# A two-layer hybrid block on one core: the RWKV scan's inverses laid out head outermost, its u through two PSUM banks, and the first modulation in parts of 768 and 512 tokens without GpSimd

## The chip, the cores and the metric

The kernel runs on one core of a Trainium2 chip. The metric is the device time of one execution in microseconds; three executions of the kernel before took 3964.69, 3973.21 and 3976.9 us (median 3973.21). In what follows, PE is TensorE (PEld its weight loads), DVE is VectorE, ACT is ScalarE, POOL is GpSimd, and SP is SyncE, which issues most of the transfers.

## The reference, cut to what matters

Two layers of a diffusion transformer work on 256 context and 1024 latent tokens of width 1024. Layer 0 mixes the tokens with an mLSTM and with RWKV-7, layer 1 with HGRN-2 and latent attention. Only the entry of layer 0 and the RWKV-7 recurrence are touched here:

```
hj = concat([modulate(rmsnorm(xc, g), shc_a, scc_a),      # 256 context tokens
             modulate(rmsnorm(x, g),  sh_a,  sc_a)])      # 1024 latent tokens
modulate(h, shift, scale) = h * (1 + scale) + shift       # per feature
feat = hj @ w_in                                          # 3984 columns
# RWKV-7, both directions, 8 heads of 64:
sa = S @ a_t
S  = S * w_t + sa b_t^T + v_t k_t^T
y_t = S @ r_t
```

The kernel computes the recurrence in chunks of 64 tokens. Within a chunk the values `sa` of all tokens depend on each other through a triangular system; its inverse, one 64x64 matrix for each head, chunk and direction, is prepared ahead of the scan.

## The kernel before, in words

The program is one long list of instructions written through a tile framework. The framework gives every tile a buffer of its pool's tag (so many buffers for each tag), orders the instructions of each engine by a priority, which follows the order in the source, and by a simulation of when each is ready, and puts semaphores between engines. The engines then work through their lists strictly in order. Two accesses to one PSUM bank by different engines are put one behind the other, even if they touch different partitions. `weave` interleaves generators: it takes one segment of each in turn, and a segment ends at a `yield`.

*The entry (lines 606 to 640).* `scaled` loads the tokens in batches of 2, 4 and 4 tiles of 128, scales each token by its norm (line 317), and transposes it on PE (line 619) into `xT`, features on partitions, tokens along the row. For each batch there are eight PSUM evictions, one for each block `k` of 128 features, all on DVE (lines 621 and 623). Beside it `ada` computes the shift and the scale of each feature (`modT`, `AT`, lines 257 and 271). The tokens are then modulated in two halves of 640. For each of the eight blocks `k` of a half: the context tokens are modulated on DVE (line 635), the latent ones on ACT (line 637); DVE rounds the result to the high part `hh` (line 639); GpSimd, or DVE where `k % 3 == 2`, subtracts it to give the low part `hl` (line 640). Every product with weights is then made of three matmuls, `hh*wh`, `hh*wl` and `hl*wh` (lines 286 to 288).

*Weights.* `prefetch` takes the next 128 columns of the input weights: a load on SP into the tile `raw` (line 280, one buffer), the high part `wh` on ACT (line 281), and the low part `wl`, here on DVE (line 282); the split tiles have two buffers. Both first prefetches stand between the two halves of the tokens. `weights` hands out what is ready and prefetches more.

*The first features.* The features 12, 13, 14, 4, 0 and 8 come first, for the first 640 tokens. Each takes two PSUM tiles (tag "ps", four buffers): tokens 0 to 256, and tokens 256 to 642 (`PART`, with two neighbours for a mean over tokens). Only then come tokens from 639 on.

*The scan (lines 983 to 1141).* Two generators, `scan(1)` and `scan(0)`, one for each direction, are woven with the remaining modulation matmuls (line 245). PSUM has tags `ch` (three buffers), `am` (three), `ps` (one) and `mo` (one). In each of ten steps `load` fetches one tile of 128 tokens (two chunks): among others the inverses `XB` (line 1017), whose two heads of a pair lie on the partitions 0 to 63 and 64 to 127, each in its own 64 of 128 columns, with zeros beside them. For each chunk: `pr` (lines 1086 and 1087) and its copy `rs` on DVE (1089); `pu`, the inverses times `rs`, eight matmuls in the source, for four pairs of heads and two heads of a pair (line 1094); the copy of `pu` into `uv`, the partitions 0 to 63 on DVE (1096) and 64 to 127 on ACT (1097); the new state `pz` (1105 and 1106) with its sum, decay and copies (1108 to 1117); the output `py` (1125 and 1127). `pr`, `pu`, `pz` and `py` all use the tag `ch`. Between them stand parts of the preparation of the next step's matrices, `products` (1034 to 1044) and `turn` (1052 to 1056, whose three copies into `KB` are on ACT). When a tile has got both directions, `finish` normalizes it (1151 to 1165).

The lines of the change:

Of the kernel before, what the change touches and what calls it, by code (L numbers as in the profile page):

```python
# [10 lines left out]
F32 = mybir.dt.float32  # L11
F32R = mybir.dt.float32r
AF = mybir.ActivationFunctionType
ALU = mybir.AluOpType
# [3 lines left out]
P = 128  # L18
# [5 lines left out]
T = NCTX + NLAT  # L24
# [131 lines left out]
def _body(tc, nc, I, out, dbg, stop, es):  # L156
    V, S, G, TE, SY = nc.vector, nc.scalar, nc.gpsimd, nc.tensor, nc.sync
# [3 lines left out]
    def nm(p):  # L161
        _n[0] += 1
        return f"{p}_{_n[0]}"
# [11 lines left out]
    def ps(w=512, tag="ps"):  # L175
        pool, bufs = banks[tag]
        t = pool.tile([P, 512], F32, tag=tag, name=nm("ps"), bufs=bufs)
        return t if w == 512 else t[:, :w]
# [4 lines left out]
    def dram(shape, name):  # L183
        return tc.dram_tile(list(shape), F32, name=name)
# [369 lines left out]
    xcd = dram([2, P, 20, 4, 64], "xcd")  # L554
# [11 lines left out]
    with ExitStack() as ph:  # L566
        lay = ExitStack()
        hp = ph.enter_context(tc.tile_pool(name="hp", bufs=1, reuse_waits="tile"))
        hh = hp.tile([P, KD, T], F32R, name="hh")
        hl = hp.tile([P, KD, T], F32R, name="hl")  # L570
# [20 lines left out]
        def prefetch():  # L591
            c0 = feats.pop(0)
            ready.append(wsplit(I["ev_w"][:, c0:c0 + P].rearrange("(k p) c -> p k c", p=P), [P, KD, P], pool=wp, bufs=2, rbufs=1, leng=V))
# [7 lines left out]
        with tc.tile_pool(name="np", bufs=2, side="right", reuse_waits="tile") as npool:  # L601
            xT = npool.tile([P, KD, T], F32, name="xT", bufs=1)

            def scaled():

                for src, i0, n, t0 in ((I["xc"], 0, 2, 0), (I["x"], 0, 4, 256), (I["x"], 4, 4, 768)):
                    xs = []
                    for i in range(n):
                        xt = npool.tile([P, D], F32, tag="xt", name=nm("xt"), bufs=4)
                        SY.dma_start(xt, src[(i0 + i) * P:(i0 + i + 1) * P, :])  # L610
                        xs.append(xt)
                    yield
                    for i, xt in enumerate(xs):
                        norm_scale(npool, xt, xt, xT[:, :, t0 + i * P:t0 + (i + 1) * P])
                    yield
                    for k in range(KD):
                        pt = ps()
                        for i, xt in enumerate(xs):
                            TE.transpose(pt[:, i * P:(i + 1) * P], xt[:, k * P:(k + 1) * P], ident)
                        if k % 2:  # L620
                            V.tensor_copy(xT[:, k, t0:t0 + n * P], pt[:, :n * P])
                        else:
                            V.tensor_copy(xT[:, k, t0:t0 + n * P], pt[:, :n * P])
                        if k % 2:
                            yield
            weave(scaled(), ada(0, npool, [0], 4))
            for t0, t1 in ((0, T // 2), (T // 2, T)):
                if t0:
                    prefetch()
                    prefetch()  # L630
                for k in range(KD):
                    for c0, c1, v in ((t0, max(t0, NCTX), 1), (max(t0, NCTX), t1, 0)):
                        m, b, f = AT[:, 0, 0, k, v:v + 1], modT[:, 0, k, v:v + 1], xT[:, k, c0:c1]
                        if v and c1 > c0:
                            V.tensor_scalar(f, f, m, b, op0=ALU.mult, op1=ALU.add)
                        elif c1 > c0:
                            S.activation(f, f, AF.Identity, bias=b, scale=m)
                    f = xT[:, k, t0:t1]
                    V.tensor_copy(hh[:, k, t0:t1], f)  # L639
                    (V if k % 3 == 2 else G).tensor_tensor(hl[:, k, t0:t1], f, hh[:, k, t0:t1], op=ALU.subtract)  # L640
        H = T // 2

        PART = (((0, 256, 0, 0, 256, 1, 1), (256, 386, 256, 0, 384, 1, 0)), ((639, 322, 0, 1, 320, 0, 0), (958, 322, 320, 2, 320, 0, 1)))
# [340 lines left out]
    with ExitStack() as ph:  # L984
        sb = ph.enter_context(ExitStack())
        sb.enter_context(psum(ch=3, am=3, ps=1, mo=1))
        rp = scans.enter_context(tc.tile_pool(name="rp", bufs=1, side="right", reuse_waits="tile"))
# [3 lines left out]
        yfd = dram([NT, P, 4, P], "yfd")  # L991
        hfd = dram([NT, P, 512], "hfd")

        XB = [[rp.tile([P, 2, 4, P], F32, name=f"XB{d}{i}") for i in range(2)] for d in range(2)]
        ZB = [[rp.tile([P, 4, P], F32, name=f"ZB{d}{i}") for i in range(2)] for d in range(2)]
        for t_ in XB[0] + XB[1] + ZB[0] + ZB[1]:
            G.memset(t_, 0.0)
# [3 lines left out]
        def scan(d):  # L1001
            bst4 = strict.unsqueeze(1).to_broadcast((P, 4, 64))

            def load(step):
                c = ORD[d][step]
                xb = XB[d][step % 2]
                CM = rp.tile([P, 4, 3, P], F32, tag="CM", name=nm("CM"), bufs=4)
                BK = rp.tile([P, 4, 2, 2, 64], F32, tag="BK", name=nm("BK"), bufs=3)
                ZV = rp.tile([P, 2, 2, 4, 64], F32, tag="ZV", name=nm("ZV"), bufs=4)
                SY.dma_start(CM[0:64, :, 0:2, :], ard[d][c, 0:64])  # L1010
                SY.dma_start(CM[64:128, :, 1:3, :], ard[d][c, 64:128])
                SY.dma_start(BK, bkd[d][c])
                for e in range(2):
                    q = slice(64 * e, 64 * e + 64)
                    SY.dma_start(ZV[64 - 64 * e:128 - 64 * e, :, e].rearrange("p c f v -> p c (f v)"),
                                 vtd[d][c * P:(c + 1) * P, e].rearrange("(c t) f v -> t c (f v)", c=2))
                    SY.dma_start(xb[q, :, :, 64 * e:64 * e + 64].rearrange("p c f t -> p (c f) t"),
                                 xcd[d, q, 2 * c:2 * c + 2].rearrange("p c f t -> p (c f) t"))
                return dict(c=c, xb=xb, CM=CM, BK=BK, ZV=ZV)

            def amat(o):
# [49 lines left out]
            for step in range(NT):  # L1071
# [4 lines left out]
                c, xb, CM, ZV, AM, KB = (cur[k] for k in ("c", "xb", "CM", "ZV", "AM", "KB"))  # L1076
                first = step < ORD[1 - d].index(c) or (step == ORD[1 - d].index(c) and d == 0)
                yt = rp.tile([P, 4, P], F32, tag=f"yt{d}", name=nm("yt"), bufs=2)
                for cc in range(2):
                    tk = slice(64 * cc, 64 * cc + 64)  # L1080
                    last = step == NT - 1 and cc == 1
                    uv, zb = ZV[:, cc], ZB[d][zi % 2]
# [5 lines left out]
                    rs = rp.tile([P, 4, 64], F32, tag="rs", name=nm("rs"), bufs=2)  # L1088
                    V.tensor_copy(rs, pr.rearrange("p (f v) -> p f v", f=4))
                    yield  # L1090
                    pu = ps(256, tag="ch")
                    for f in range(4):
                        for e in (0, 64):
                            TE.matmul(pu[e:e + 64, f * 64:f * 64 + 64], xb[:, cc, f, e:e + 64], rs[:, f, :], start=True, stop=True)
                    puv = pu.rearrange("p (f v) -> p f v", f=4)
                    V.tensor_copy(uv[0:64, 0], puv[0:64])
                    S.copy(uv[64:128, 1], puv[64:128])
                    if parts:
                        parts.pop(0)()
                    yield  # L1100
                    if not last:
# [5 lines left out]
                        t1 = rp.tile([P, 4, 64], F32, tag="t1", name=nm("t1"), bufs=2)  # L1107
# [77 lines left out]
        def gates_ml():  # L1185
# [90 lines left out]
            yield  # L1276

        weave((gates_ml(), 1, 0), (scan(1), 1, 0), (scan(0), 1, 0), (mods, 0.6, 0))
        scans.close()
        sb.close()  # L1280
# [167 lines left out]
    with both as ph:  # L1448
# [5 lines left out]
        for f in (4, 5, 6, 7, 8, 9, 10, 11, 0, 1, 2, 3):  # L1454
# [7 lines left out]
            for r in runs[1:] if f < 4 else runs:  # L1462
                pt = held.pop(1) if f == F0 and r in runs[:2] else od_run(w, *r)
                next(mods, None)
                t0, n = r[:2]
# [8 lines left out]
            else:  # L1474
                d = f // 4 - 1
# [544 lines left out]
```

## Time and profile before

| what | value |
|---|---|
| median of three executions | 3973.21 us (3964.69 to 3976.9) |
| the profiled execution | 3966.18 us, span 3964.4 us |
| PE busy | 3620.1 us, 91% |
| DVE, ACT, POOL busy | 57%, 35%, 38% |
| mean granted clock of PE | 0.956 |
| 0 to 90 us: loading, scaling and modulating the first tokens | PE full only from about 89 us |
| 768 to 1082 us: the scan | PE busy 261.88 of 314 us |

The page of the profile has the busy time of each engine, the span in 40 slices with the busy share of each in tenths, and the costliest groups of instructions by line. A view of stretches gives the busy time of each engine in each stretch of time, the granted clock and the share of time the transfers were busy. A row of a group has the line, the engine, the operation, out and in, the shapes, the count, the busy time and the mean of one in ns, and the idle time of the engine ahead of it with what ended it. A row of waits reads: who waited for whom, us in total, times, longest. A row of the timeline starts with the start and the length in us. The view of one line gives the shortest, the median and the longest of its instructions in ns. Times count from the start of the span.

### The profile page before, as it was taken

Reading aid. Unit: us, or ns where it says so; the run is one execution under the profiler, and the core shown is the slowest. Engines: PE = TensorE matmul, PEld = TensorE weight load, DVE = VectorE, ACT = ScalarE, POOL = GpSimd, SP = SyncE. Lnnn points to the kernel's source line nnn. Section 1 sums busy time; section 2 is a strip of 40 time slices with the busy share of each in tenths; the row PEclk is TensorE's granted clock in tenths of the full one; section 3 lists DMA queues with packets and bytes.
Section 4 is the critical chain, followed back from the end, with each engine's and each line's share of the span. In section 5 each row is a group of like instructions: output and inputs, shape, how many; then the busy total and the mean of one; then the engine's idle time right before and its main releaser. Section 6 shows DMA issues by size and latency. Waiting matters only on the chain.

```text
span 3964.4 us, 66839 instructions
## 1 busy us (share of the span) xinstructions
PE 3620.1 (91%) x26934; PEld 3104.0 (78%) x26934; DVE 2266.7 (57%) x3627; ACT 1368.7 (35%) x2641; POOL 1506.0 (38%) x1532
## 2 busy tenths in 40 slices
PE   5999989888778799999999989989888979999998
PEld 3888879766667598998999878986666758888887
DVE  6564653355566656556655542227777466666655
ACT  3444342355533432123312142224444444223221
POOL 3044646433343443233323231234455544333332
PEclk7999999899889899999999999999999989999999
DMA  4555646779587633223222266322122364334332
GB/s 169 125 136 127 158 124 160 186 196 247 165 288 238 213 91 96 75 80 117 76 74 80 70 205 203 114 94 89 61 81 84 101 206 123 101 96 139 95 101 75
DMA packets 534911, 521.32 MB, mean 132 GB/s; under 512 B 128297, under 2 KB 443625, under 8 KB 534601
## 3 DMA queue, kind: packets, MB, share of 16 engines
q1 hardware_dynamic: 438904, 441.03, 38.1%
q10 hardware_dynamic: 82080, 35.17, 3.1%
q0 software_dynamic: 13616, 40.84, 2.9%
q8 instruction: 212, 3.47, 0.4%
q14 instruction: 99, 0.80, 0.1%
HBM read 395.79 MB, written 121.16 MB: 130 GB/s over the span
## 4 chain that ended last, share of the span: by engine, by line
PE 51%; DVE 6%; POOL 4%; DMA 3%; issue 2%; ACT 2%; POOLq 0%; SPq 0%; DVEq 0%; ACTq 0%
PE ps L286 16%; PE ps L287 16%; PE ps L288 16%; POOL tb L1685 1%; DMA raw<-in_mlp_w 1%; DVE KQ L1690 1%; DVE el L1883 1%; POOL wl L282 1%; POOL acc L1885 0%; PE ps L245 0%; DVE acc L504 0%; ACT wh L281 0%; DMA y<-yd 0%; POOL mh L338 0%; PE ps L1848 0%
## 5 line engine op out<-in xcount | busy, mean ns | idle before, releaser
L281 ACT CAST wh<-raw 128x1024 fp32r<-128x1024 f32 x330 | 340.9, 1049 | 1002.0 <-PE ps L288 497.4
L286 PE MATMUL ps<-mh,wh 128*128 128x384 f32 (+2 forms) x1888 | 631.2, 334 | 4.7 <-ACT mh L337 3.0
L288 PE MATMUL ps<-mh,wl 128*128 128x256 f32 (+2 forms) x1888 | 627.6, 332 | 3.3 <-POOL wl L282 3.3
L287 PE MATMUL ps<-mh,wh 128*128 128x256 f32 (+2 forms) x1888 | 627.6, 332 | 0.0
L471 DVE TENSOR_TENSOR relu<-relu 128x384 f32<-128x384 f32 (+1 forms) x192 | 332.9, 1734 | 398.8 <-ACT relu L470 398.7
L282 POOL TENSOR_TENSOR wl<-raw,wh 128x1024 fp32r<-128x1024 f32 x145 | 350.9, 2421 | 534.7 <-ACT wh L281 533.2
L286 PE MATMUL ps<-wh,h1h 128*128 128x512 f32 x1152 | 451.1, 392 | 5.4 <-ACT acc L502 2.7
L288 PE MATMUL ps<-wh,h1l 128*128 128x512 f32 x1152 | 449.9, 391 | 0.0
L287 PE MATMUL ps<-wl,h1h 128*128 128x512 f32 x1152 | 449.6, 390 | 0.0
L504 DVE TENSOR_TENSOR acc<-ps,acc 128x512 f32<-128x512 f32 x540 | 359.4, 685 | 153.8 <-PE ps L288 151.0
L473 POOL TENSOR_TENSOR h1l<-relu,h1h 128x384 fp32r<-128x384 f32 (+1 forms) x192 | 202.8, 1056 | 531.1 <-DVE h1h L472 527.4
L286 PEld LDWEIGHTS ps<-mh,wh 128*128 128x128 f32 x1888 | 358.2, 190 | 39.0 <-issue 11.1
L288 PEld LDWEIGHTS ps<-mh,wl 128*128 128x128 f32 x1888 | 358.0, 190 | 23.7 <-POOL wl L282 3.8
L287 PEld LDWEIGHTS ps<-mh,wh 128*128 128x128 f32 x1888 | 358.0, 190 | 21.6 <-POOL mh L338 0.3
L282 DVE TENSOR_TENSOR wl<-raw,wh 128x1024 fp32r<-128x1024 f32 x185 | 235.9, 1299 | 210.3 <-ACT wh L281 190.1
L288 PE MATMUL ps<-hh,wl 128*128 128x256 f32 (+2 forms) x992 | 315.8, 318 | 14.6 <-DVE wl L282 14.6
L286 PE MATMUL ps<-hh,wh 128*128 128x256 f32 (+2 forms) x992 | 324.4, 327 | 3.6 <-DVE hh L639 3.6
L287 PE MATMUL ps<-hl,wh 128*128 128x256 f32 (+2 forms) x992 | 317.7, 320 | 5.4 <-POOL hl L640 5.0
L286 PEld LDWEIGHTS ps<-wh,h1h 128*128 128x128 f32 x1152 | 216.8, 188 | 50.8 <-DVE acc L504 3.7
L288 PEld LDWEIGHTS ps<-wh,h1l 128*128 128x128 f32 x1152 | 216.8, 188 | 45.3
L287 PEld LDWEIGHTS ps<-wl,h1h 128*128 128x128 f32 x1152 | 216.9, 188 | 43.5 <-DVE wl L282 0.2
L288 PEld LDWEIGHTS ps<-hh,wl 128*128 128x128 f32 x992 | 192.9, 194 | 15.9 <-DVE wl L282 15.4
(533 smaller groups left out, 7288.9 us busy)
## 6 DMA issues: line engine op xcount, KB each, us to landing
raw<-in_mlp_w SPq DMA_DIRECT2D x256, 512.0 KB, 4.0
adaw<-in_ada_w SPq DMA_DIRECT2D x96, 512.0 KB, 4.5
raw<-in_ev_w SPq DMA_DIRECT2D x46, 512.0 KB, 4.0
bkd<-BK SPq DMA_DIRECT2D x16, 640.0 KB
CM<-ard SPq DMA_DIRECT2D x40, 256.0 KB, 9.1
BK<-bkd SPq DMA_DIRECT2D x20, 512.0 KB, 8.6
qk<-qkd SPq DMA_DIRECT2D x20, 512.0 KB, 7.9
fk<-fkd SPq DMA_DIRECT2D x20, 512.0 KB, 4.3
```

The source lines that it names most:

```text
L281: S.copy(h, raw)
L282: (leng or G).tensor_tensor(l, raw, h, op=ALU.subtract)
L286: TE.matmul(o, lh, rh, start=first, stop=False)
L287: TE.matmul(o, lh, rl, start=False, stop=False)
L288: TE.matmul(o, ll, rh, start=False, stop=last)
L471: V.tensor_tensor(r_, r_, r_, op=ALU.mult)
L473: G.tensor_tensor(l_[:, t0:t1], r_, a[:, t0:t1], op=ALU.subtract)
L504: V.tensor_tensor(acc[i][:, cs_], pt, acc[i][:, cs_], op=ALU.add)
L1685: G.tensor_tensor(nx, cb[:, :, 0], cb[:, :, 1], op=ALU.mult)
L1690: V.tensor_tensor(o, o, w, op=ALU.mult)
L1883: (V, V, V, G)[k % 4].tensor_tensor(el, e, eh, op=ALU.subtract)
```

## The change

It has three edits. (1) In the entry, the evictions of odd blocks move from DVE to ACT; the tokens are modulated in parts of 768 and 512 instead of 640 and 640; one prefetch stands ahead of the first part and one ahead of the second; the high parts are rounded on ACT except where `k % 4 == 3`, which stay on DVE; all the subtractions are on DVE. (2) The tile `XB` has the head outermost, so that what one partition loads for one head is one piece of 2 KB, where it was eight of 256 bytes. The zeros beside it stay zero. (3) The products of the two heads of a pair go to two PSUM tiles, one of tag `ch` and one of tag `ps`; DVE reads one, ACT the other.

```diff
                         if k % 2:
-                            V.tensor_copy(xT[:, k, t0:t0 + n * P], pt[:, :n * P])
+                            S.copy(xT[:, k, t0:t0 + n * P], pt[:, :n * P])
                         else:
                             V.tensor_copy(xT[:, k, t0:t0 + n * P], pt[:, :n * P])
...
-            for t0, t1 in ((0, T // 2), (T // 2, T)):
+
+            prefetch()
+            for t0, t1 in ((0, 768), (768, T)):
                 if t0:
-                    prefetch()
                     prefetch()
                 for k in range(KD):
...
                     f = xT[:, k, t0:t1]
-                    V.tensor_copy(hh[:, k, t0:t1], f)
-                    (V if k % 3 == 2 else G).tensor_tensor(hl[:, k, t0:t1], f, hh[:, k, t0:t1], op=ALU.subtract)
+                    if k % 4 == 3:
+                        V.tensor_copy(hh[:, k, t0:t1], f)
+                    else:
+                        S.copy(hh[:, k, t0:t1], f)
+                    V.tensor_tensor(hl[:, k, t0:t1], f, hh[:, k, t0:t1], op=ALU.subtract)
...
-        XB = [[rp.tile([P, 2, 4, P], F32, name=f"XB{d}{i}") for i in range(2)] for d in range(2)]
+        XB = [[rp.tile([P, 2, 2, 4, 64], F32, name=f"XB{d}{i}") for i in range(2)] for d in range(2)]
...
-                    SY.dma_start(xb[q, :, :, 64 * e:64 * e + 64].rearrange("p c f t -> p (c f) t"),
-                                 xcd[d, q, 2 * c:2 * c + 2].rearrange("p c f t -> p (c f) t"))
+                    SY.dma_start(xb[q, e].rearrange("p c f t -> p (c f t)"), xcd[d, q, 2 * c:2 * c + 2].rearrange("p c f t -> p (c f t)"))
...
-                    pu = ps(256, tag="ch")
+
+                    pus = [ps(256, tag=t_).rearrange("p (f v) -> p f v", f=4) for t_ in ("ch", "ps")]
                     for f in range(4):
-                        for e in (0, 64):
-                            TE.matmul(pu[e:e + 64, f * 64:f * 64 + 64], xb[:, cc, f, e:e + 64], rs[:, f, :], start=True, stop=True)
-                    puv = pu.rearrange("p (f v) -> p f v", f=4)
-                    V.tensor_copy(uv[0:64, 0], puv[0:64])
-                    S.copy(uv[64:128, 1], puv[64:128])
+                        for e, pu in enumerate(pus):
+                            TE.matmul(pu[64 * e:64 * e + 64, f], xb[:, e, cc, f, :], rs[:, f, :], start=True, stop=True)
+                    V.tensor_copy(uv[0:64, 0], pus[0][0:64])
+                    S.copy(uv[64:128, 1], pus[1][64:128])
```

## The prediction

> **What bounds the kernel now.** I read the page first, then the prologue and the scan in stretches of time, their waits and their groups of instructions. TensorE (PE) carries the kernel, so an edit is worth what it takes from PE's idle time in its own stage.
>
> ```profile
> PE 3620.1 (91%) x26934; PEld 3104.0 (78%) x26934; DVE 2266.7 (57%) x3627; ACT 1368.7 (35%) x2641; POOL 1506.0 (38%) x1532
> PE   5999989888778799999999989989888979999998
> ```
>
> The slices (99 us each) dip at the start, where the first tokens are modulated, and in slices 8 to 13, of which 8 to 11 hold the scan. The diff touches just these two places. First the prologue; columns are busy time of PE, PEld, DVE, ACT, POOL, then granted clock and DMA share:
>
> ```profile
> 56.50:69.50 13.00, 1.14 (x2) 0.58 (x2) 13.00 (x21) 11.39 (x16) 7.29 (x5) 0.55 0.01 1
> 69.50:72.00 2.50, 0.00 (x0) 0.00 (x0) 2.50 (x2) 0.00 (x0) 1.39 (x1) 0.50 0.00 0
> 72.00:76.20 4.20, 4.18 (x24) 4.18 (x25) 4.20 (x4) 0.24 (x1) 3.75 (x3) 0.65 0.46 125
> 76.20:89.10 12.90, 8.22 (x26) 5.27 (x26) 12.86 (x19) 1.29 (x2) 8.90 (x5) 0.72 0.15 41
> 89.10:97.50 8.40, 8.40 (x50) 8.40 (x50) 3.86 (x7) 2.94 (x5) 0.00 (x0) 0.83 0.29 79
> 97.50:104.60 7.10, 7.10 (x51) 7.10 (x50) 3.34 (x5) 2.01 (x4) 0.00 (x0) 1.00 0.30 76
> ...
> PE ps L288 <- DVE wl L282: 10.8, 1, 10.8
> ...
> PE ps L287 <- POOL hl L640: 5.0, 5, 1.3
> ...
> PE ps L286 <- DVE hh L639: 3.6, 2, 3.1
> ```
>
> VectorE (DVE) is busy without a break from 56.5 to 89.1 while PE mostly waits. The first feature needs 24 matmuls over 256 columns and 24 over 386 (tokens 256 to 642). The former run from 72.0 to 76.2, since the first weights' low part (L282) comes behind the whole first half of tokens. The latter need tokens past 640, so they crawl to 89.1 behind the second half. From 89.1 PE is full, and a feature takes 7.1 us at full clock. Why DVE is so slow:
>
> ```profile
> L639 DVE CAST hh<-xT x16: 479/482/1857, 58.3 to 85.9; 128x640 fp32r<-128x640 f32 x16
> ...
> L635 DVE TENSOR_SCALAR xT<-xT,AT,modT x8: 400/1016/1634, 57.7 to 69.1; 128x256 f32<-128x256 f32 x8
> ...
> L639 DVE CAST hh<-xT 128x640 fp32r<-128x640 f32 x16 | 13.8, 905 | 0.0
> L635 DVE TENSOR_SCALAR xT<-xT,AT,modT 128x256 f32<-128x256 f32 x8 | 7.9, 1016 | 0.0
> L282 DVE TENSOR_TENSOR wl<-raw,wh 128x1024 fp32r<-128x1024 f32 x2 | 5.1, 2558 | 0.0
> L640 DVE TENSOR_TENSOR hl<-xT,hh 128x640 fp32r<-128x640 f32 x4 | 3.2, 812 | 0.0
> ...
> L640 POOL TENSOR_TENSOR hl<-xT,hh 128x640 fp32r<-128x640 f32 x12 | 21.3, 1786 | 16.1 <-DVE hh L639 16.1
> ...
> L282 DVE TENSOR_TENSOR wl<-raw,wh 128x1024 fp32r<-128x1024 f32 x185 | 235.9, 1299 | 210.3 <-ACT wh L281 190.1
> ```
>
> The same cast takes 0.48 or 1.86 us, the same scaling 0.40 or 1.63, and L282 2.56 here against 1.30 over the run. The long ones are those beside GpSimd's twelve subtractions. Against minima and means that is (0.905-0.48)x16 + (1.016-0.40)x8 + (2.558-1.299)x2 = 14 us of DVE time in this stretch.
>
> **The prologue after the change.** ScalarE (ACT) has these rows to price its new work; L1054 is a PSUM copy of the scan, taken as the nearest row for an eviction:
>
> ```profile
> 50.87 1.05 ACT L281 CAST wh<-raw 128x1024 fp32r<-128x1024 f32 x1 [1.30 <-DMA raw<-in_ev_w]
> 56.50 11.39 ACT L637 ACTIVATE xT<-xT,modT,AT 128x384 f32<-128x384 f32 x16 [4.38 <-DVE AT L271]
> ...
> L637 ACT ACTIVATE xT<-xT,modT,AT 128x640 f32<-128x640 f32 x8 | 6.6, 906 | 0.0
> L637 ACT ACTIVATE xT<-xT,modT,AT 128x384 f32<-128x384 f32 x8 | 4.9, 694 | 4.4 <-DVE AT L271 4.4
> ...
> L1054 ACT COPY KB<-ps 128x512 f32<-128x512 f32 x20 | 11.7, 586 | 1.6 <-PE ps L1052 1.0
> ...
> L621 DVE COPY xT<-ps 128x512 f32<-128x512 f32 x8 | 5.5, 685 | 1.1 <-PE ps L619 1.1
> ```
>
> Evictions: 12 of 24 go from DVE to ACT. In the last batch of tokens that is 4x0.59 = 2.4 us of ACT, in the 4.38 us that it idles before L637, and 4x0.685 = 2.7 us off DVE, where the scales (L271) stand behind most of the copies. I take 1 us of that as gain (bounds 0 and 2.7: the transposes may set the pace). The first 8 lie beside loads; nothing taken.
>
> First part, 768 tokens, on DVE: one L282 1.3, eight scalings 8x0.40 = 3.2, two casts of 768 2x0.48x768/640 = 1.2, eight subtractions 8x0.812x768/640 = 7.8: 13.5 us. On ACT: two L637 rows give 0.83 ns a column, so eight of 512 cost 8x0.80 = 6.4, and six casts of 768 (1.05 less 256 columns) 6x0.84 = 5.0: 11.4 us. DVE sets the pace. It began at 56.5 and now begins at 55.5, plus 1 us until the first cast from ACT arrives: the part is ready at 70, where it was ready before with 640 tokens. No GpSimd runs, so the short durations hold.
>
> PE takes the 256-column matmuls with DVE, token block by token block, instead of behind it; the last pair ends at 70.5. The 386-column ones then have all their tokens: 386/642 of 7.1 = 4.3 us at full clock, 8.5 at half. PE will have been busy some 30% of the time before (4.2 us of matmuls in 13.5), and a dense start got 0.65 over its first 4.2 us (72.0 to 76.2), which leaves 4.3-2.7 = 1.6 us for after: 5.8 us, end 76.3. The second feature follows at full clock until 83.4, against 97.5 before. Gain **14 us**. Bounds: 0, if DVE and ACT wait for each other at each block (below); 19, if the overlap of consecutive DVE instructions and the evictions each give 2 us more and the clock is full.
>
> The Trainium skill, page "TensorE: Matmul & The Clock Gate", section "What's actually happening", says that half rate is the idle state and that one busy window of about 3.4 us brings full rate; the 0.65 above agrees. Should the paced stretch count as busy there, the 386-column matmuls would run at full rate at once and the gain were 15.5.
>
> The later part, 512 tokens, is 8x0.65 + 2x0.39 = 6 us of DVE and 8x0.80 + 6x0.63 = 10.2 us of ACT. It is hidden under six features at tokens below 642, 6x7.1 = 43 us of PE; without that cover it would cost its 10 us. On ACT and DVE the features' own evictions queue behind it, but four PSUM buffers hold two features. Weights: of the two loads issued between the parts one now stands ahead of the first; its DMA and cast ran ahead already (50.87), so only its L282 moves, past the whole first part. The raw tile has one buffer, so the second load waits on SP for that L282, now some 15 us earlier; nothing is moved past POOL's queue. After the prologue PE is the bound (7.10 of 7.10), so I carry the gain to the end.
>
> **The scan after the change.**
>
> ```profile
> 768.00:1082.00 314.00, 261.88 (x4484) 205.68 (x4484) 166.31 (x364) 166.28 (x353) 111.41 (x111) 0.91 0.80 208
> ...
> ACT ZV L1097 <- DVE ZV L1096: 44.0, 22, 8.1
> ...
> PE ps L1105 <- DVE ZV L1096: 10.1, 3, 3.9
> ...
> PE ps L1094 <- ACT ZV L1097: 3.1, 3, 1.0
> PE ps L1105 <- ACT ZV L1097: 3.1, 3, 1.0
> ...
> L1096 DVE COPY ZV<-ps 64x256 f32<-64x256 f32 x40 | 16.5, 414 | 21.6 <-PE ps L1094 18.2 <-ACT KB L1056 2.3 <-ACT ZV L1097 0.3
> ...
> 904.27 1.15 PE L1094 MATMUL ps<-rs,XB 128*64 128x64 f32 x32
> 905.07 0.88 DVE L1096 COPY ZV<-ps 64x256 f32<-64x256 f32 x2 [0.82 <-PE ps L1094]
> ...
> 905.58 0.83 ACT L1097 COPY ZV<-ps 64x256 f32<-64x256 f32 x2 [4.78 <-DVE ZV L1096]
> ```
>
> Both copies of u read one bank, and ACT's waits for DVE's. Two banks let it start 0.414 + 0.1 (905.58 less the first copy's end) = 0.5 us earlier. But ACT's 44 us of waiting are not PE's: PE waits six times for L1097, and the three long waits for L1096 stay. Six times 0.5 is 3 us; 44.0 us of ACT counted 22 times at 0.5 bounds it at 11.
>
> The change adds a wait. The second bank is the tag "ps", one buffer, and both directions use it. The second direction's matmuls into it wait until the first's L1097 has read it: u of both was one run of 32 matmuls in 1.15 us, and now a gap of about 0.1+0.37+0.1 = 0.57 stands in its middle (0.83 for two of ACT's copies is 0.37 each with 0.1 between). Behind it in PE's queue are the state's products (L1105) and the modulation matmuls. Where the rounds' u's are back to back, that costs 0.1 to 0.6; in others the second one is later anyway. I take 8 of 20 rounds at 0.3 = 2 us. Bounds: 0 and 24 (below). Net gain 1 us.
>
> The XB load has 256-byte pieces and 128 KB, and becomes 2 KB pieces:
>
> ```profile
> ZV<-vtd SPq DMA_DIRECT2D x35, 128.0 KB, 7.7
> ...
> XB<-xcd SPq DMA_DIRECT2D x36, 128.0 KB, 7.7
> ```
>
> ZV of the same size with 1 KB pieces lands as late, so I take 0. The Trainium skill, "DMA: Bandwidth & Descriptors", section "Specifications", puts line rate at 512 bytes and more; these two rows show no such difference in landing.
>
> **Sum.** The profiled execution took 3966.2 us (span 3964.4 and 1.8 around it); less 14 and 1 it is 3951. It lies 7 below the median of the runs shown, so the predicted median is 3973.2 - 15 = **3958**. About 0.3%, 11.9 us, is what a measurement can tell from no change.
>
> **Rivals.**
> *Lockstep in the prologue.* If each block goes strictly scaling, ACT's modulation, ACT's cast, subtraction, it costs 0.40+0.80+0.84+0.97 = 3.0 us, eight of them 24 instead of 12, and the gain is 2; halfway, 8. For it: ACT now has two steps in each block's chain. Against it: the blocks are independent, and before ACT ran its 16 modulations in one go. Median 3965 to 3971, say 3968.
> *The one "ps" buffer as a turnstile (slower).* In each step ACT has six KB copies like L1054, 3.5 us, ahead of L1097. If they delay the first u's release while the second u stands at the head of PE's queue, ten rounds lose about 1.8 and ten 0.6: 24 us, median 3973 - 14 + 24 = 3983. For it: PE works in order and was 83% busy (261.88 of 314) here. Against: PE's idle time often lies at this very place. It decides from 0.7 us a round (no gain left), and from 1.3 it is over 0.3%.
> *Relief of the DMA queues in the scan.* DMA is 0.80 busy there with 314x208 GB/s = 65 MB; XB's 36 loads there are 4.7 MB, 7%. If short pieces cost twice and the DMA were the bound, half of 2x7% would go, 0.80x314x0.07 = 18 us; I price it at 12: median 3946. Against: PE's large waits above name DVE and ACT.
>
> **How the numbers follow.** Forecast 0.57 (its own range 3950 to 3966), lockstep 0.20, turnstile 0.13, relief 0.10. Range 3944 to 3977: it leaves out half of the turnstile and some of the relief. Faster by over 0.3% (below 3961.3): 0.46 of the forecast, relief, 0.02 of lockstep: 0.58. Slower (above 3985.1): half of the turnstile, 0.07. Within: 0.35.
>
> **What would show it.** In the profile after: no GpSimd subtraction before 100 us, L635 and DVE's hh casts all short; the first L288 near 57 instead of 72; PE's full stretch from about 70 and the second feature done near 83; L1097 no longer waiting for L1096 but for L1094; idle time before L1094 named after L1097 if the turnstile bites. I am wrong if PE is full only after 80, or if the 314 us of the scan change by more than 10.

## The result, and the profile after

The change makes the kernel faster: the median of four executions is 3940.55 us (3935.91 to 3946.24), that of four of the kernel before 3975.06 us; the ratio is 0.9913, with a 95% interval of 0.9894 to 0.9932. That is 34.5 us, 27 to 42 by the interval. I had predicted 3958 (3944 to 3977). The direction was right; the time lies below the range. Part of the 34.5 is the sample of the kernel before: over the 11 to 29 executions beside each set of experiments its median was 3968.75 to 3971.79, and against these the change is worth some 30 us.

The profiled execution after took 3941.64 us (span 3939.6). First its page: the busy time of each engine and the slices.

```profile
PE 3615.9 (92%) x26934; PEld 3102.5 (79%) x26934; DVE 2248.7 (57%) x3615; ACT 1381.5 (35%) x2665; POOL 1488.7 (38%) x1520
...
PE   6989989888788799999999989989888979999998
```

PE does the same 26934 matmuls and is busy for 4 us less; most of the 24.8 us between the two spans is idle time. The stretches of the prologue, in the columns used before:

```profile
56.50:69.50 13.00, 9.89 (x49) 9.38 (x50) 12.96 (x22) 13.00 (x20) 0.00 (x0) 0.74 0.15 43
69.50:72.00 2.50, 2.50 (x22) 2.50 (x21) 1.81 (x5) 2.50 (x6) 0.00 (x0) 1.00 0.46 112
72.00:76.20 4.20, 4.20 (x28) 4.20 (x27) 2.86 (x5) 4.20 (x7) 0.00 (x0) 1.00 0.19 58
76.20:89.10 12.90, 8.50 (x46) 8.21 (x45) 9.29 (x23) 5.14 (x9) 0.00 (x0) 0.74 0.35 93
89.10:97.50 8.40, 8.40 (x54) 7.87 (x53) 3.34 (x5) 4.63 (x7) 0.00 (x0) 1.00 0.24 62
```

Three shorter stretches say more of the clock:

```profile
60.50:65.10 4.60, 4.59 (x17) 4.59 (x18) 4.60 (x7) 4.60 (x8) 0.00 (x0) 0.50 0.08 23
65.10:69.50 4.40, 4.40 (x31) 4.29 (x31) 4.37 (x7) 4.40 (x8) 0.00 (x0) 1.00 0.00 0
...
81.10:85.50 4.40, 4.35 (x20) 4.38 (x21) 3.48 (x6) 1.79 (x2) 0.00 (x0) 0.50 0.25 73
```

PE works without a break from 60.5 on, at half clock up to 65.1 and at full clock behind it. Then comes something I had not drawn: a hole between 76.2 and 89.1. The timeline of PE and DVE there (start, length, instruction, idle time before it and what ended it):

```profile
76.41 0.34 PE L288 MATMUL ps<-hh,wl 128*128 128x386 f32 x1
81.15 0.55 PE L286 MATMUL ps<-hh,wh 128*128 128x256 f32 x1 [4.40 <-DVE twl L725]
```

```profile
76.33 1.29 DVE L644 TENSOR_TENSOR hl<-xT,hh 128x512 fp32r<-128x512 f32 x2
77.54 1.22 DVE L282 TENSOR_TENSOR wl<-raw,wh 128x1024 fp32r<-128x1024 f32 x1
78.68 0.17 DVE L785 TENSOR_SCALAR sm<-pp 128x15 f32<-128x15 f32 x1
...
79.53 1.09 DVE L723 SCALAR_TENSOR_TENSOR twl<-ps,sm,twl 128x255 f32<-128x255 f32 x2
```

The second feature ends at 76.75 (97.54 before). Then all four PSUM buffers hold products that nobody has read: the evictions (L721 to L725) need the factors `sm`, and DVE comes to these only behind the last subtraction of the second part (L644) and one L282. PE waits 4.4 us and then runs at half clock up to 85.5 (the last of the three stretches above), so the third feature ends at 90.42, against 104.63 before. The gain is 20.8 us after two features and 14.2 after three; it stays between 14.1 and 14.3 up to 270 us, and between 12 and 16 up to 350.

The scan, between the same two matmuls as the stretch of 314 us before, and three of its waits:

```profile
753.10:1050.20 297.10, 262.04 (x4489) 206.53 (x4488) 168.21 (x371) 167.00 (x356) 111.40 (x111) 0.95 0.77 219
```

```profile
ACT ZV L1100 <- PE ps L1098: 23.2, 20, 2.7
...
PE ps L1108 <- DVE ZV L1099: 7.7, 9, 2.2
...
PE ps L1098 <- ACT ZV L1100: 4.3, 5, 1.0
```

297 us instead of 314: 17 less, where I had priced 1. The two edits do what their lines say: ACT's copy no longer waits for DVE's, and the shared second bank holds PE up five times. Neither row is worth 17 us. That sum is what the experiments had to explain. (Where the scan is over, at PE's 9600th matmul, the kernel after is 32.2 us ahead in these two executions, and at the end of the span 24.8; what takes the rest back is open.)

### The profile page after: what moved, and what is told of

The parts are those of the page before. It is cut to its first block, busy times and chain, and to the rows that moved or that the text cites. A ratio compares the mean times of both kernels' runs of the same rounds, so it can differ in the third digit from the quotient of the medians.

```text
span 3939.6 us, 66858 instructions
## 1 busy us (share of the span) xinstructions
PE 3615.9 (92%) x26934; PEld 3102.5 (79%) x26934; DVE 2248.7 (57%) x3615; ACT 1381.5 (35%) x2665; POOL 1488.7 (38%) x1520
## 4 chain that ended last, share of the span: by engine, by line
PE 51%; DVE 6%; POOL 3%; DMA 3%; issue 2%; ACT 2%; SPq 0%; POOLq 0%; DVEq 0%; ACTq 0%
PE ps L286 16%; PE ps L287 16%; PE ps L288 16%; DVE KQ L1693 1%; POOL tb L1688 1%; DMA raw<-in_mlp_w 1%; DVE el L1886 0%; POOL wl L282 0%; POOL acc L1888 0%; PE ps L245 0%; PE ps L1851 0%; DVE acc L504 0%; DVE x L400 0%; PE ps L1645 0%; DMA q<-qhd 0%
## 5 line engine op out<-in xcount | busy, mean ns | idle before, releaser
L282 POOL TENSOR_TENSOR wl<-raw,wh 128x1024 fp32r<-128x1024 f32 x145 | 351.3, 2423 | 533.3 <-ACT wh L281 530.8
L282 DVE TENSOR_TENSOR wl<-raw,wh 128x1024 fp32r<-128x1024 f32 x185 | 232.8, 1282 | 207.2 <-ACT wh L281 200.1
L287 PE MATMUL ps<-hl,wh 128*128 128x322 f32 (+3 forms) x992 | 315.5, 318 | 0.1
L286 PEld LDWEIGHTS ps<-hh,wh 128*128 128x128 f32 x992 | 192.5, 195 | 14.9 <-ACT al L721 4.7
```

The source lines that it names most:

```text
L282: (leng or G).tensor_tensor(l, raw, h, op=ALU.subtract)
L286: TE.matmul(o, lh, rh, start=first, stop=False)
L287: TE.matmul(o, lh, rl, start=False, stop=False)
```

## The experiments

All ratios are against the kernel before on the same chip, with 95% intervals. 1% is 39.7 us.

### Which edit carries what

The entry alone; both edits of the scan alone; the layout of `XB` alone (u in one bank); u through two banks alone (`XB` with its pieces of 256 bytes).

> The entry of the change alone; the scan as before. Theory 1 (the two copies of u side by side: the scan gains by itself, some 0.4 us in each of its 40 half steps) and theory 2 (relief of the DMA queues by the larger pieces of XB): the entry is worth the 14 us seen in the prologue, so 3961 against 3975, ratio 0.9965. Theory 3 (what was gained in the scan is a matter of timing: the earlier start lets loads and the work woven in fall elsewhere): most of the 34 us comes with the entry, 3945 to 3950, ratio 0.993.

> Both edits of the scan (XB by heads, u through two banks); the entry as before. Theories 1 and 2: 13 to 20 us gained, 3955 to 3962, ratio 0.9955. Theory 3: at most 5 us, 3970 or more.

> XB laid out and loaded with the head outermost (2 KB pieces), u in one bank in the old order; the entry as before. Theory 1: within 3 us of before, 3972 to 3978. Theory 2: 12 us or more gained, 3963 or less, and PE's named waits for the loads in the scan fall while ACT still waits some 44 us for DVE's copy of u.

> u through two banks alone, XB with its old 256-byte pieces; the entry as before. Theory 1: nearly all of the scan's gain, 12 to 17 us, 3958 to 3963; the copies of u start together and the idle time of PE in the scan falls by 15 us. Theory 2: within 3 us of before. The turnstile (both directions share the one second bank) would show as a loss: 3980 or more.

The layout alone is the tile, its load, and the index of the product:

```diff
-        XB = [[rp.tile([P, 2, 4, P], F32, name=f"XB{d}{i}") ...
+        XB = [[rp.tile([P, 2, 2, 4, 64], F32, name=f"XB{d}{i}") ...
-                            TE.matmul(pu[e:e + 64, ...], xb[:, cc, f, e:e + 64], rs[:, f, :], ...)
+                            TE.matmul(pu[e:e + 64, ...], xb[:, e // 64, cc, f, :], rs[:, f, :], ...)
```

| kernel | median us | ratio | interval |
|---|---|---|---|
| entry | 3955.45 | 0.9971 | 0.9955 to 0.9986 |
| both scan edits | 3955.79 | 0.9962 | 0.9950 to 0.9974 |
| layout | 3948.06 | 0.9947 | 0.9928 to 0.9966 |
| two banks | 3968.63 | 1.0005 | 0.9993 to 1.0016 |

The entry is worth 11.5 us, near the 14 of the prologue. My first theory, that the two copies of u running side by side had gained the 17 us, falls: two banks alone are worth nothing. The gain in the scan comes with the layout. (Layout alone and both edits can't be told apart: their intervals overlap.) That looked like the rival that I had given 0.10, relief of the queues.

### The layout: the pieces, or the order of the lists

The layout changes two things. It makes the pieces longer on the chip, and it makes the framework's simulation plan anew. In the two built programs 1219 of the 2464 PE instructions of the scan stand at another place in PE's list, 142 of 416 on DVE and 139 of 365 on ACT; SP's list is the same. So I pinned the lists. After the scan is written, each engine's instructions are chained, without any wait, in the order of the other program:

```diff
+        for x, y in zip(q, q[1:]):          # q: one engine's instructions of the scan, in the other program's order
+            tc.add_manual_dep(traced[y], x, free, reason="pin")
```

> The layout alone (2 KB pieces), but each engine's list in the scan pinned, instruction by instruction, to the order that the framework made for the kernel before. The two kernels then differ in nothing but the pieces of the transfer and the place of XB in its tile. If the layout's 21 us are relief of the queues on the chip: about 15 to 21 us gained, 3950 to 3956. If they are the order (the framework's simulation takes XB to land earlier and so sets 1219 of PE's 2464 instructions in other places): within 4 us of before, ratio 0.999 to 1.001.

> The kernel before with its 256-byte pieces, its lists in the scan pinned to the order that the framework made for the layout alone. If the gain is relief of the queues: no gain, and a loss of up to 5 us where instructions placed early wait for XB in the list: 3971 to 3976. If it is the order: about 21 us gained, 3950, ratio 0.9947.

The layout in the old order: 3966.62 us, ratio 0.9989 (0.9979 to 1.0000). The kernel before, 256-byte pieces and all, in the new order: 3954.11 us, ratio 0.9956 (0.9942 to 0.9970). The gain is the order. The pieces themselves are worth some 4 us in the old order, 0 to 8 by the interval.

### Where in the order

The gaps between copies of u show it. DVE makes 40 of them (L1096), and I call the time from one to the next a round, by the number of the copy that ends it. The rounds agree within a few us in most cases. Three stand out, all in steps that end with `finish`:

| round | before | layout, old order | before, new order | layout | whole change |
|---|---|---|---|---|---|
| 29 | 29.9 | 30.6 | 22.6 | 22.6 | 24.2 |
| 33 | 28.0 | 28.0 | 29.0 | 25.2 | 24.3 |
| 37 | 29.5 | 29.5 | 22.9 | 22.9 | 24.3 |

Round 37, in which the queues are nearly idle, as stretches of the kernel before, of the layout in the old order, and of the kernel before in the new order:

```profile
1040.00:1069.60 29.60, 21.47 (x256) 16.22 (x256) 12.72 (x28) 17.80 (x30) 8.25 (x8) 0.80 0.07 19
1040.00:1046.30 6.30, 4.15 (x64) 3.66 (x64) 3.56 (x7) 1.98 (x5) 1.71 (x2) 0.57 0.00 0
```

```profile
1037.40:1067.00 29.60, 21.48 (x256) 16.23 (x256) 12.70 (x28) 17.81 (x30) 8.24 (x8) 0.80 0.06 19
```

```profile
1033.40:1056.30 22.90, 16.61 (x256) 12.37 (x255) 13.33 (x27) 17.81 (x30) 8.37 (x8) 0.91 0.08 24
```

The same 256 matmuls take 29.6 or 22.9 us, and which of the two goes with the order and not with the pieces. The timeline of PE in the kernel before says what stands there:

```profile
1039.24 0.69 PE L1094 MATMUL ps<-rs,XB 128*64 128x64 f32 x16 [1.04 <-ACT ZV L1097]
1040.96 0.37 PE L1105 MATMUL ps<-ZV,KB 128*64 128x64 f32 x1 [1.04 <-ACT ZV L1097]
...
1041.12 0.31 PE L1105 MATMUL ps<-ZV,KB 128*64 128x64 f32 x1
...
1042.68 0.37 PE L1105 MATMUL ps<-ZV,KB 128*64 128x64 f32 x1 [0.59 <-DVE t L1108]
...
1044.40 0.48 PE L1125 MATMUL ps<-CM,ZB 128*64 128x64 f32 x4 [0.60 <-DVE t L1108]
...
1046.30 0.59 PE L1034 MATMUL ps<-CM,BK 64*128 64x128 f32 x2
```

PE takes the new state (L1105) first, waits for the copies of u and then for the state's sum, three times in a row, and comes to the products of the next step's matrices (L1034), which need none of this, 6.3 us into the round. ACT's copies of those products and of the matrices turned behind them (L1039 to L1056, some 7 of its 17.8 us in this round) come later by as much. One rule would mend it: in the second half of a step the state's products stand behind the products of the next step.

```diff
+                        if cc:
+                            behind = last_on(tc, mybir.EngineType.PE)      # the last product (L1034) just written
...
+                            if behind and f == 0:
+                                tc.add_manual_dep(z_.ins, behind.name, FREE, reason="z behind the products")
```

> The kernel before with one rule for the order: in the second half of each step, the products for the state (L1105) of a direction stand on PE behind the products of its next step's matrices (L1034); the rest of the order is the framework's. If the gain of the new order is that these products fill PE while the copies of u run, instead of standing behind the state: the rounds 29, 33 and 37 between copies of u fall from 28 to 30 us to 23 to 25, and 10 to 17 us are gained, 3953 to 3960, ratio 0.996 to 0.9975. If the gain is spread over the other thousand places: within 4 us of before; if the state now waits for work that it doesn't need, slower.

The kernel before with this rule alone: 3951.41 us, ratio 0.9956 (0.9940 to 0.9972), 17.5 us, as much as the whole new order. Its rounds 29, 33 and 37 take 22.6, 23.3 and 22.9 us. The stretch of round 37 and the timeline of PE (the rule shifts the lines by 8 to 11: L1042 is L1034 of before, L1116 is L1105):

```profile
1025.60:1048.50 22.90, 16.23 (x256) 11.97 (x254) 13.34 (x28) 17.81 (x30) 8.42 (x8) 0.92 0.18 62
```

```profile
1024.76 0.69 PE L1102 MATMUL ps<-rs,XB 128*64 128x64 f32 x16 [1.04 <-ACT ZV L1105]
1025.38 4.46 PE L1042 MATMUL ps<-CM,BK 64*128 64x128 f32 x48
1029.77 0.27 PE L1116 MATMUL ps<-ZV,KB 128*64 128x64 f32 x1
...
1029.87 0.22 PE L1116 MATMUL ps<-ZV,KB 128*64 128x64 f32 x1
```

The products fill the 4.4 us in which the copies run, and the state finds them done. That is what the rule does in the rounds 33 and 37, which go from 57.5 us together to 46.2.

Round 29 is another case. There the kernel before has the products behind u already, and PE waits later, ahead of modulation matmuls (L245), for their weights:

```profile
958.34 4.46 PE L1034 MATMUL ps<-CM,BK 64*128 64x128 f32 x48
962.72 0.27 PE L1105 MATMUL ps<-ZV,KB 128*64 128x64 f32 x1
```

```profile
PE ps L245 <- DMA adaw<-in_ada_w: 2.6, 3, 1.1
```

Under the rule this wait is gone and the round is 7.3 us shorter; how one leads to the other is not shown.

The whole change has an order of its own, which I did not pin. In its rounds 33 and 37 the state still comes first, with two of the three waits, and the products fill the third, ahead of the outputs (L1108 is L1105 of before, L1037 is L1034):

```profile
1013.35 0.27 PE L1108 MATMUL ps<-ZV,KB 128*64 128x64 f32 x1 [0.58 <-DVE ZV L1099]
...
1014.63 0.27 PE L1108 MATMUL ps<-ZV,KB 128*64 128x64 f32 x1 [0.60 <-DVE t L1111]
...
1015.24 4.46 PE L1037 MATMUL ps<-CM,BK 64*128 64x128 f32 x48
```

Nor is the time saved in the same way. From the first copy of u to the last, in the kernel before, under the rule and in the whole change:

```profile
775.70:1078.80 303.10, 251.23 (x4328) 196.22 (x4326) 162.54 (x356) 159.90 (x338) 107.60 (x108) 0.92 0.80 208
```

```profile
775.60:1057.90 282.30, 237.91 (x4328) 185.75 (x4326) 164.97 (x355) 158.93 (x338) 107.86 (x108) 0.97 0.83 223
```

```profile
761.50:1046.30 284.80, 249.74 (x4331) 195.60 (x4329) 164.47 (x363) 160.89 (x342) 107.58 (x108) 0.96 0.77 220
```

Of the rule's 20.8 us, 7.5 are idle time of PE, and 13.3 are the same matmuls keeping PE busy for less time, at a granted clock of 0.97 instead of 0.92. Of the 18.3 us of the whole change, 16.8 are idle time; why PE is busy there for as long as before, at 0.96, stays open.

### The rule with the rest, and the banks once more

> The entry and the layout, u in one bank as before. If the two gains add (11.5 measured for the entry alone, 21 for the layout alone): 3938, ratio 0.992. If the second bank costs after the layout what the layout alone has over both scan edits (3948 against 3956), this version is 3 to 8 us faster than the whole change: 3933 to 3938. If the second bank is worth something beside the layout, it is slower than the whole change: 3943 or more.

> The entry and the layout with the same rule for the second half of each step. If the framework's order has already what the rule gives: within 4 us of the entry and the layout alone (3937). If other steps gain too: 3925 to 3932, faster than both kernels. If the rule holds up the state where it has no wait to fill: 3942 or more.

> The whole change with the rule for the order (in the second half of a step the state's products behind the next step's products). Beside the entry and the layout under the same rule (3937.8, ratio 0.9918) it differs in the second bank alone. If two banks are worth the 0.5 us per wait that I saw, six waits or more: 3 to 8 us faster, 3930 to 3935. If the one buffer of the second bank takes back what the copies gain: within 4 us, 3935 to 3942.

> The whole change with the second bank of u in two buffers instead of one (the tag of the prepared products gives one of its three). If the shared buffer is a turnstile that matters: PE's 10.7 us of named waits for ACT's copy at the products of u go, and 4 to 8 us are gained on the whole change, 3933 to 3937. If it doesn't matter: within 3 us of the whole change; if the products miss their third buffer, slower, 3945 to 3955.

> The entry and the rule for the order, and neither of the change's edits of the scan (256-byte pieces, one bank). If the whole change is worth its entry and its new order: 0.9971 x 0.9956 = 0.9927, 3940 to 3943, within 4 us of the whole change. If the layout or the bank has a price of its own beside them: 3946 or more.

> The same entry and the same order of the scan, instruction by instruction, as the kernel with entry and rule, but XB in pieces of 2 KB. If the pieces are worth 2 to 7 us on the chip at a given order, as the two pairs of pinned kernels had it: 3934 to 3938, the fastest so far. If they are worth nothing: within 2 us of entry and rule.

The edits are those shown above, put together; the two buffers are `psum(ch=3, am=2, ps=2, mo=1)` in place of `psum(ch=3, am=3, ps=1, mo=1)`; the last one is the entry and the layout, pinned to the order of the kernel before with the rule.

| kernel | median us | ratio | interval |
|---|---|---|---|
| whole change | 3940.55 | 0.9913 | 0.9894 to 0.9932 |
| entry, layout | 3937.29 | 0.9918 | 0.9903 to 0.9934 |
| entry, layout, rule | 3937.79 | 0.9918 | 0.9900 to 0.9935 |
| whole change, rule | 3942.29 | 0.9932 | 0.9917 to 0.9946 |
| whole change, two buffers | 3960.74 | 0.9975 | 0.9965 to 0.9986 |
| entry, rule (no layout, one bank) | 3937.84 | 0.9924 | 0.9907 to 0.9941 |
| entry, layout, order of the rule | 3935.96 | 0.9923 | 0.9906 to 0.9940 |

Entry and rule, without either edit of the scan, give what the whole change gives; 0.9971 x 0.9956 = 0.9927 was expected. At a held order the longer pieces show nothing (the last two rows). The second bank is worth nothing that can be seen: with the rule, two banks stand at 0.9932 and one at 0.9918, and the intervals overlap. Two buffers for it lose some 20 us on the whole change. From the first copy of u to the last it takes 306.4 us instead of 284.8. The prepared products then have two buffers instead of three, and in round 37 their matmuls come in groups of 16 between others instead of 48 in a row; but that round is not longer (22.4 us), the loss lies in other rounds, and its cause is not shown. What the turnstile itself costs can't be read from that run. The rule adds nothing to an order that the framework planned with the longer pieces. It shortens the rounds 29, 33 and 37 of the whole change to 20.9, 22.3 and 22.9 us, but others grow, and from the first copy of u to the last it is 287.2 us instead of 284.8. Apart from the one with two buffers, none of these versions can be told from the whole change.

### The entry

GpSimd's subtractions put back into the whole change; its parts made 640 and 640; one weight load moved ahead in the kernel before; both loads put between the parts in the whole change; and in the kernel before all subtractions on DVE, nothing else changed.

```diff
-                    V.tensor_tensor(hl[:, k, t0:t1], f, hh[:, k, t0:t1], op=ALU.subtract)
+                    (V if k % 3 == 2 else G).tensor_tensor(hl[:, k, t0:t1], f, hh[:, k, t0:t1], op=ALU.subtract)
```

```diff
-            for t0, t1 in ((0, 768), (768, T)):
+            for t0, t1 in ((0, T // 2), (T // 2, T)):
```

```diff
+            prefetch()
             for t0, t1 in ((0, T // 2), (T // 2, T)):
                 if t0:
                     prefetch()
-                    prefetch()
```

> The whole change, but in the entry GpSimd takes back the subtractions of the low parts (all but each third block), as before; parts of 768 and 512 and the evictions stay. If the entry's gain is the contention of DVE with GpSimd: the casts and scalings on DVE take 1 us and more again, PE is full only from 80 us or later, 10 us or more are lost, 3950. If it is the boundary at 768 and the weights loaded ahead: the first part is late by GpSimd's own 2.1 us a block only, PE is full from 72 to 74, at most 5 us lost.

> The whole change, but the tokens in halves of 640 as before; ACT's evictions and casts stay, no GpSimd. If the entry's gain is the contention alone: the second half of the tokens follows within 10 us without long instructions, and at most 4 us are lost, 3941 to 3945. If the boundary matters (the first feature's columns to 642 need the second half): its 386-column matmuls end behind the second half's eight blocks, about 8 us later, 3948.

> The kernel before, with one of the two weight loads moved ahead of the first half of the tokens, and nothing else. If the place of the first weights' low part carries what GpSimd (5 us of 14) and the boundary (0 of 14) left open: the wait of 10.8 us goes, the first feature's 256 columns are done by 70, but its 386 columns still end with the second half at 88: 4 to 9 us gained in the prologue, 3960 to 3965. If DVE's length decides alone: PE is full from 88 to 89 as before, at most 2 us gained, 3967 to 3972.

> The whole change, with both weight loads between the two parts of the tokens, as before. If the place of the weights carries the open 9 us: PE waits some 10 us for the low part, and 4 to 9 us of the entry's gain go, 3944 to 3949. If DVE's length decides alone: the low part comes behind 13 us of DVE instead of 26, PE is full from 72, and at most 3 us go, 3940 to 3943.

> The kernel before with all sixteen subtractions of the low parts on DVE and none on GpSimd; casts and evictions stay on DVE. By the prediction's step (14 us of long instructions go, twelve more subtractions of 0.81 us come, 9.7 us): 4 to 5 us gained in the prologue, 3964 to 3968. If GpSimd's company was not what made DVE slow: 10 us lost, 3980.

| kernel | median us | ratio | interval | prologue: ahead of before at 128 us |
|---|---|---|---|---|
| whole change | 3940.55 | 0.9913 | 0.9894 to 0.9932 | 14.3 |
| with GpSimd again | 3950.83 | 0.9951 | 0.9934 to 0.9969 | 9.4 |
| with 640 and 640 | 3941.95 | 0.9929 | 0.9913 to 0.9946 | 14.2 |
| with both loads between | 3941.24 | 0.9926 | 0.9905 to 0.9947 | 14.9 |
| before, one load ahead | 3967.06 | 0.9995 | 0.9981 to 1.0008 | 1.0 |
| before, no GpSimd | 3964.90 | 0.9982 | 0.9966 to 0.9999 | 10.8 |

The last column is the end of PE's 500th matmul, in the one profiled execution of each. Among the runs with the entry of before it lies between 125.64 and 128.25, and among those with the whole entry between 111.17 and 114.53, so a difference of some 3 us says nothing. Boundary and place of the loads are worth nothing at that point. The boundary does help the first features: with 640 and 640 the second ended at 82.08 instead of 76.75, but the third at 90.54 and not 90.42, since the hole takes all of it. With both loads written between the parts PE had the low part in time all the same (its 48th feature matmul ended at 68.92); with one load ahead in the kernel before, the wait of 10.8 us was gone, but DVE was as long as ever and PE as late. GpSimd's subtractions moved to DVE alone give 10.8 us, where I had expected 4 to 5; what makes the difference stays open. The rest of the entry, with GpSimd, gives 9.4, and both together 14.3, so the two gains overlap. DVE's groups without GpSimd, in the same code as before otherwise:

```profile
L640 DVE TENSOR_TENSOR hl<-xT,hh 128x640 fp32r<-128x640 f32 x16 | 12.4, 814 | 0.0
L639 DVE CAST hh<-xT 128x640 fp32r<-128x640 f32 x16 | 7.1, 483 | 0.0
L282 DVE TENSOR_TENSOR wl<-raw,wh 128x1024 fp32r<-128x1024 f32 x5 | 6.1, 1223 | 4.8 <-ACT wh L281 4.7
L635 DVE TENSOR_SCALAR xT<-xT,AT,modT 128x256 f32<-128x256 f32 x8 | 2.9, 404 | 0.0
```

The two casts of DVE in the whole change, and with GpSimd put back into it:

```profile
L641 DVE CAST hh<-xT 128x768 fp32r<-128x768 f32 x2 | 1.1, 552 | 0.0
L641 DVE CAST hh<-xT 128x512 fp32r<-128x512 f32 x2 | 0.9, 426 | 1.3 <-ACT xT L638 1.3
```

```profile
L641 DVE CAST hh<-xT 128x512 fp32r<-128x512 f32 x2 | 2.6, 1325 | 0.8 <-ACT xT L638 0.8
L641 DVE CAST hh<-xT 128x768 fp32r<-128x768 f32 x2 | 2.5, 1240 | 0.2 <-ACT xT L638 0.2
```

Same cast, same shape: 905 ns in the mean beside GpSimd before, 483 without it; the scalings 1016 and 404; L282 2558 and 1223. That GpSimd makes DVE slow is shown by taking it away and by putting it back. The Trainium skill, "SBUF — State Buffer", section "SBUF: two separate sides", says that the two share a pair of ports and that the loser is blocked for the other's whole instruction, not slowed in proportion. The casts of the kernel before agree: half of them took 482 ns or less, the longest 1857.

## Why the prediction was wrong in size, step by step

**DVE's contention, 14 us of its time.** Right, and now shown (483 for 905, 404 for 1016, 1223 for 2558).

**The prologue's gain, 14 us.** Its size came out at 14.3, by way of two errors that cancel. The first part was ready at 70 as said, but the framework did not set the 386-column matmuls behind the 256-column ones: it interleaved them block by block, so the second feature ended at 76.75 and not at 83.4. Then 4.4 us were lost in the hole and 2.2 more to the half clock after it (the third feature took 9.3 us, from 81.15 to 90.42, instead of 7.1). My sentence that four PSUM buffers hold two features was true and missed the point: the third needs an eviction, and evictions begin only behind the second part. PE wasn't paced to some 30% either: it worked without a break from 60.5, and full clock came at 65.1, ahead of the end of the first part. The rule of the Trainium skill that I weighed ("TensorE: Matmul & The Clock Gate", section "What's actually happening") is that one busy window of about 3.4 us brings full rate, in windows that run on whatever the kernel does; the 4.6 us here agree with it. Whether a paced stretch counts as busy, this trace can't say. The 15.5 us that I had worked out for full clock were not reached, because of the hole.

**The boundary and the loads.** I tied the first feature's gain to the boundary at 768 and the low part L282 to its new place. The boundary gives the second feature 5 us, which are gone at the third, and the place of the load gives nothing.

**The scan, net 1 us.** This is the step that failed, and it makes the miss: 17 us measured where 1 was priced, and 3958 less these 16 is 3942. The prediction's own sign of being wrong, a scan that changes by more than 10 us, came true. Its two terms were sound where I looked: two banks alone measured nothing (1.0005, 0.9993 to 1.0016), which fits the 3 less 2 that I had given them. I treated the lists of the engines as fixed, and priced an edit only by the waits beside its own lines. The text before the prediction says that the framework orders the lists by a simulation; a load with other pieces is another input to it. The state's products and the next step's were free to change places, and PE's waits between L1094, L1105 and L1125 were there to be filled. For the layout alone the order is shown to be the cause; that it is also what gains the 17 us of the whole change is inferred, from the equal times of the entry with the layout and of the entry with the rule. That the simulation moved them *because* it takes XB's longer pieces to be cheaper is argued from the layout alone having changed the order; I did not look into it.

**XB's pieces, 0 us.** Nearly right: some 4 us in the old order, nothing that can be seen in the new. The Trainium skill, "DMA: Bandwidth & Descriptors", section "Specifications", has 512 bytes as the smallest transfer at full rate. The queues did have less to do (a share of 0.80 busy in the 314 us before, 0.77 in the 297 after), but PE's named waits for a load were the 2.6 us of round 29 alone, and with the longer pieces in the old order they were still there (2.8 us).

**The rivals.** The relief rival had the right edit and nearly the right time (3946), with the wrong mechanism: the same longer pieces in the old order give 4 us. Turnstile: PE waited 4.3 us in all. Lockstep: it didn't come.

**The offset.** I put the profiled execution 7 us below the median; over more executions of the kernel before it is 3 to 6. (And the dip of the slices runs from 8 to 14, not to 13; nothing hung on it.)

## What to carry to other kernels

Where a framework plans the order, an edit of a transfer or a tile is also a new plan: price what the engine could do in the waits of the stage, not only the waits beside the edit, and pin the order when you want to know what an edit itself is worth. On an engine that works in order, work that needs nothing from the recurrence belongs into the recurrence's waits, ahead of what waits; one rule to that effect was worth 17 us here, and nothing on an order that had already gained as much. When a first stage is sped up, look at who must read its results next.

## What was not expected of the hardware

Short waits can cost more than their length. In the first 6.3 us of round 37 PE stood idle for three waits of 1.04, 0.59 and 0.60 us, the granted clock was 0.57, and a matmul of the state took 0.31 us; behind the products, at 0.92 over the round, it took 0.22. Of the 6.7 us that the order gains there, PE's busy time fell by 5.2 (21.47 to 16.23) for the same matmuls, and its idle time by only 1.5. It need not be so: in the same round of the whole change PE waited for 0.58 and 0.60 us ahead of the state, the granted clock stayed at 1.00, and the matmul took 0.22:

```profile
1012.90:1015.20 2.30, 1.26 (x30) 1.09 (x30) 1.38 (x4) 0.14 (x1) 0.55 (x1) 1.00 0.00 0
```

In the new order with 256-byte pieces round 33 took 29.0 us at a granted clock of 0.76, and with 2 KB pieces in the same order 25.2. Entry and rule, in short and in long pieces, took 23.1 us each in that round. The round in short pieces, and behind it the one in long pieces:

```profile
991.90:1020.90 29.00, 24.35 (x288) 18.41 (x288) 12.67 (x27) 17.71 (x30) 7.95 (x8) 0.76 0.77 214
```

```profile
985.50:1010.70 25.20, 20.52 (x288) 15.03 (x288) 12.65 (x27) 17.71 (x30) 7.99 (x8) 0.93 0.84 245
```

The same 288 matmuls kept PE busy for 24.35 us and for 20.52, and this is the whole difference between the two rounds; their idle time is the same, 4.65 and 4.68. So the round was long in PE's own pace, at the lower clock. Why the clock was lower there stays open.
